# Moving one layer's hyena filter into its own layer in a two-layer encoder kernel

## The chip, the core and the metric

The kernel runs on one core of a Trainium2 chip. The metric is the device time of one execution in microseconds (us), from three runs, beside one profiled execution whose trace is read here. The names of the engines are those of the profile: PE (TensorE matmul) and PEld (its weight loads), DVE (VectorE), ACT (ScalarE), POOL (GpSimd), SP (SyncE, which here only issues loads).

## What is computed

Two requests ("streams" 0 and 1 below) of 512 tokens by 1024 channels go through two layers. The part of the reference that matters, cut:

```python
def _hyena_filters(L, w1, b1, freq, w2, b2, w3):       # depends on weights only, not on x
    feats = jnp.concatenate([t, jnp.cos(w), -jnp.sin(w)], axis=-1)          # 512 x 33
    h = jnp.sin(fr * (feats @ w1 + b1))                                     # 512 x 64
    h = jnp.sin(fr * (h @ w2 + b2))                                         # 512 x 64
    h = (h @ w3).reshape(L, HY_ORDER, 2, HY_WIDTH)                          # 512 x 1024
    h = h * jnp.exp(-t[:, :, None, None] * deltas)
    ...
    k_full = k_full / jnp.sum(jnp.abs(k_full), axis=0, keepdims=True)
    return jnp.fft.rfft(k_full, axis=0)

def _layer(x, p, ...):
    h = _rmsnorm(x, norm_mix)
    q, k, v, g, hy_in, pool_in = jnp.split(h @ w_in, ...)
    ret = _head_layernorm(_retention(q, k, v, ret_decay_fwd, ret_decay_bwd)) * silu(g)   # 4 heads of 128
    hy_out = _hyena(hy_in, ...)       # two long convolutions by FFT with the filters, 256 channels
    pool_out = _pool_mixer(pool_in, ...)
    x = x + jnp.concatenate([ret, hy_out, pool_out], -1) @ w_out
    gate, up = jnp.split(_rmsnorm(x, norm_ffn) @ ffn_w_up, 2, axis=-1)
    x = x + (gelu(_dwconv3(gate, ffn_conv)) * up) @ ffn_w_down
    return x + jax.nn.sigmoid(x @ ple_gate_w) * _rmsnorm(p @ ple_w, ple_norm)
```

The retention multiplies scores by a decay table exp(dist * log_sigmoid(logit)), one per head and layer, which also depends on weights only.

## The kernel before

Activations are held transposed, 128 channels by 512 tokens in a tile. Nearly every product is made in three float16 passes: both operands are split into a high and a low half (`split`: ACT writes the high half, DVE the low one), and high by high, high by low and low by high are summed. A projection of one 128-wide output tile is 24 matmuls. Weights arrive as `wraw` and are split into `wspl`.

One layer is a mixing block and a feed-forward block. In the mixing block the tiles come by `tile_order` (L100): four of retention's values (`v00` to `v11`, tiles `vp`), then head by head a query, a key and a gate (`q0`, `k0`, `g0`, ...), and between the heads the six hyena tiles `hy0` to `hy5` and the two pooling tiles `pl0`, `pl1`. Then come the eight tiles of the output projection, `o`, which contract over `mixr` (retention, four tiles), `mixh` (hyena, two) and `mixp` (pooling, two). The feed-forward block does both streams at once by a Strassen-like scheme (`fx`, `fy`, `fz`, `ex`, `ey`, `ez`).

The order of the instructions on PE and on SP is written out by hand. A planner in `schedule` runs generator threads: `main_thread` of each stream, and threads that they spawn, `head_thread` (scores `sc`, output `ov`, then sums of squares by `cs` and their broadcast by `rb`), `hyena_thread` (`tp` to token order, `sp` to the spectrum, products with the filter, `iv` back), `pool_thread`, `decay_thread` and `filter_thread`. A thread says after each step how long its next one should stay away (the table `LAT`); the planner takes the thread that is due on its own rough clock, which is no measured time, and what it emits first stands first on PE and on SP. The order on DVE, ACT and POOL is made by the framework's scheduler from the same program. Each engine takes its instructions strictly in its order.

`filter_thread` (L461) makes a layer's filter: features to 64 rows (`fp<-feats`), a sine, 64 rows again (`fp<-fa`), a sine, then eight products with `w3s` (the split of `w3`) with decay (`hfb`), absolute values (`fabs`) and their sum (`ftot`), one product with ones, a reciprocal (`frec`), folds (`fold`, `folds`), and nine products with cosine and sine matrices (`fp<-folds,fmat`), whose results are the tiles `khat`. A sine (L445) takes six DVE instructions of argument reduction on tile `fa` and its helper `sk`, then ACT's Sin. Layer 0's filter is started at the start. Layer 1's is started in layer 0, when stream 0 comes to `EARLY`, the tile `pl1`; its nine `khat` tiles are stored to DRAM (`ksp`) and loaded again in layer 1 by `load_dft` (L667).

`decay_thread` (L424) makes the decay tables: `log_sigmoid` (some 26 DVE instructions on 128x8), then eight sets of two DVE instructions and an Exp on tiles `dect`, each stored to DRAM. For layer l it is due at 25 + 400 l on the planner's clock, which puts layer 1's at the end of layer 0's mixing block.

The lines in the rows are those of these functions: L340 to L342 are the three passes of `pass3`, L335 to L337 those of `mm3`, L179 an ACT activation, L182, L185 and L189 the vector helpers, L766 `cs`, L776 `rb`.

Of the kernel before, what the change touches and what calls it, by code (L numbers as in the profile page):

```python
# [16 lines left out]
F32 = mybir.dt.float32  # L17
F16 = mybir.dt.float16
# [5 lines left out]
T = 512  # L24
# [27 lines left out]
EARLY = "pl1"  # L52
# [28 lines left out]
    "sin": (14.0, 17.0),  # L81
}
# [64 lines left out]
ORDERS = [tile_order(l in TWINNED) for l in range(DEPTH)]  # L147
# [7 lines left out]
class Trunk:  # L155
# [227 lines left out]
    def consts(self):  # L383
# [18 lines left out]
        self.ksp = self.dr.tile([9, 128, T], F32, name="ksp")  # L402
# [58 lines left out]
    def filter_thread(self, l, ev):  # L461
        nc, io = self.nc, self.io
        ft = self.g(name="feats")
        self.load(ft[0:33, :], io["feats"])
        fw = self.g(name="fw")
        self.load(fw[0:64, 0:132], io["fw"][l])
        w3 = []
        for o in range(2):
            w = self.g(name="w3")
            self.load(w[0:64, :], io["w3"][l][:, o * T:(o + 1) * T])  # L470
            q = self.g([128, 2, T], F16, name="w3s")
            self.split(q[0:64, 0], q[0:64, 1], w[0:64, :], WS)
# [4 lines left out]
        w1, w2, b1, fr, b2 = fw[0:33, 0:64], fw[0:64, 64:128], fw[0:64, 128:129], fw[0:64, 129:130], fw[0:64, 130:131]  # L477
        yield 0.0, 0.0
        a = self.g(name="fa")
        p = self.bank(name="fp")  # L480
        nc.tensor.matmul(p[0:64, :], w1, ft[0:33, :], start=True, stop=True)
        self.ts(a[0:64, :], p[0:64, :], b1, fr, ALU.add, ALU.mult)
        self.sine(a[0:64, :])
        yield 0.9, LAT["sin"][l > 0]
        a2 = self.g(name="fa2")
        p = self.bank(name="fp")
        nc.tensor.matmul(p[0:64, :], w2, a[0:64, :], start=True, stop=True)
        self.ts(a2[0:64, :], p[0:64, :], b2, fr, ALU.add, ALU.mult)
        self.sine(a2[0:64, :])
        a = None  # L490
        h2 = self.g([128, 2, T], F16, name="h2")
        self.split(h2[0:64, 0], h2[0:64, 1], a2[0:64, :])
        yield 0.9, LAT["sin"][l > 0]
# [62 lines left out]
        for i, (kind, pr, src) in enumerate(use):  # L556
# [19 lines left out]
        if l == 0:  # L576
            self.take_filters(kh)
# [993 lines left out]
```

## Time and profile before

| | |
|---|---|
| median of 3 runs | 2455.81 us (2454.49 to 2456.82) |
| profiled execution | 2456.78 us |
| its span, first to last instruction | 2455.0 us |
| PE busy | 2382.4 us, 97% |
| DVE busy | 1782.4 us, 73% |
| ACT busy | 1031.8 us, 42% |
| POOL busy | 710.3 us, 29% |
| PE's granted clock, mean | 0.989 |

The profiled execution lasted 1.78 us longer than its span. PE is busy nearly always, so the places where it is not are few and can be listed one by one; a timeline of PE gives, in square brackets, how long it stood idle before an instruction and which instruction on which engine ended the idle time. After a stop the granted clock is for a while at half (0.5 in the units of the profile, 1.2 of 2.4 GHz), which a view by windows shows as a mean under 1.

### The profile page before, as it was taken

How to read it: one execution, taken by the hardware profiler on the slowest of the kernel's cores; microseconds unless marked ns; L12 is line 12 of the kernel's file. 1: busy time of each engine (PE TensorE's matmuls, PEld its weight loads, DVE VectorE, ACT ScalarE, POOL GpSimd, SP SyncE). 2: the span in 40 equal slices, each digit the busy share in tenths (PEclk: the TensorE clock that was granted, in tenths of full speed). 3: DMA queues.
4: the chain of work that ended last, by engine and by line, in shares of the span. 5: the costliest groups of instructions: out<-in, count | busy, mean ns of one | idle time of the engine just before them, and what ended most of it. 6: DMA issues, size and time to landing. Idle time of an engine off the chain costs nothing.

```text
span 2455.0 us, 30870 instructions
## 1 busy us (share of the span) xinstructions
PE 2382.4 (97%) x12024; PEld 1172.0 (48%) x12024; DVE 1782.4 (73%) x2526; ACT 1031.8 (42%) x1551; POOL 710.3 (29%) x528
## 2 busy tenths in 40 slices
PE   5999999899999999999999999999999999999997
PEld 3544654444444444444456555544444444444443
DVE  7894886868877868866575686464887786986655
ACT  4553334334534525443533343332453453544441
POOL 1213343113333334330121223520423434332011
PEclk8999999999999999999999999999999999999999
DMA  6121020331121121113232111032012112111301
GB/s 225 65 98 62 25 75 11 117 129 43 50 64 60 50 71 48 60 52 114 72 127 91 67 45 51 35 115 65 18 55 66 57 47 69 54 58 52 112 1 69
DMA packets 64363, 168.60 MB, mean 69 GB/s; under 512 B 7574, under 2 KB 13718, under 8 KB 64216
## 3 DMA queue, kind: packets, MB, share of 16 engines
q1 hardware_dynamic: 58312, 156.40, 19.4%
q10 hardware_dynamic: 5904, 10.23, 1.1%
q8 instruction: 94, 1.54, 0.3%
q14 instruction: 53, 0.43, 0.1%
HBM read 152.18 MB, written 14.42 MB: 68 GB/s over the span
## 4 chain that ended last, share of the span: by engine, by line
PE 69%; DVE 7%; issue 2%; POOL 1%; ACT 1%; POOLq 0%; DVEq 0%; ACTq 0%
PE fx L1265 14%; PE ex L1265 7%; PE fy L1265 7%; PE ey L1265 4%; PE fz L1265 4%; PE s L335 2%; PE s L337 2%; PE s L336 2%; PE o L336 2%; PE ez L1265 2%; PE o L337 2%; PE o L335 2%; DVE conv L182 1%; PE d L335 1%; PE d L336 1%
## 5 line engine op out<-in xcount | busy, mean ns | idle before, releaser
L1265 PEld LDWEIGHTS <-wspl 128*128 128x128 f16 x4704 | 460.3, 98 | 559.1 <-issue 4.5
L185 POOL TENSOR_TENSOR wraw<-wraw 128x512 f32<-128x512 f32 (+1 forms) x240 | 350.2, 1459 | 641.1 <-DVE wspl L182 627.0
L179 ACT ACTIVATE wspl<-wraw 128x1024 f16<-128x1024 f32 (+2 forms) x360 | 326.8, 910 | 367.7 <-POOL wraw L185 76.0
L182 DVE SCALAR_TENSOR_TENSOR wspl<-wraw,wspl 128x1024 f16<-128x1024 f32 (+2 forms) x360 | 395.1, 1099 | 86.2 <-ACT wspl L179 84.8
L1265 PE MATMUL fx<-hs,wspl 128*128 128x512 f16 x1368 | 309.0, 379 | 3.6 <-ACT r L179 3.6
L335 PEld LDWEIGHTS <-wspl 128*128 128x128 f16 x1536 | 152.3, 99 | 182.3 <-issue 8.3
L337 PEld LDWEIGHTS <-wspl 128*128 128x128 f16 x1536 | 150.7, 98 | 184.5 <-issue 4.6
L336 PEld LDWEIGHTS <-wspl 128*128 128x128 f16 x1536 | 150.8, 98 | 183.3 <-issue 10.1
L1265 PE MATMUL ex<-at,wspl 128*128 128x512 f16 x846 | 192.7, 379 | 0.0
L185 POOL TENSOR_TENSOR y<-t,mhalf 128x4 f32<-128x4 f32 x30 | 38.7, 1290 | 411.1 <-DVE t L189 411.0
L179 ACT ACTIVATE at<-conv 128x512 f16<-128x512 f32 x142 | 88.4, 628 | 124.1 <-DVE conv L185 93.3
L182 DVE SCALAR_TENSOR_TENSOR conv<-r,scaled,conv 128x511 f32<-128x511 f32 x152 | 138.6, 912 | 2.4 <-ACT conv L179 0.8
L185 DVE TENSOR_TENSOR at<-conv,at 128x512 f16<-128x512 f32 x142 | 120.8, 854 | 23.3 <-ACT at L179 22.0
L179 ACT ACTIVATE conv<-conv 128x512 f32<-128x512 f32 x88 | 55.4, 629 | 126.5 <-DVE conv L182 125.4
L1265 PE MATMUL fx<-h,wspl 128*128 128x512 f16 x456 | 104.6, 379 | 0.0
L1265 PE MATMUL fy<-hs,wspl 128*128 128x512 f16 x456 | 104.6, 379 | 0.0
L1265 PE MATMUL fz<-h,wspl 128*128 128x512 f16 x456 | 104.6, 379 | 0.0
L1265 PE MATMUL fy<-h,wspl 128*128 128x512 f16 x456 | 104.6, 379 | 0.0
L179 ACT ACTIVATE sq<-x 128x512 f32<-128x512 f32 x80 | 49.0, 624 | 127.7 <-DVE x L182 69.3
L1265 PE MATMUL ey<-at,wspl 128*128 128x512 f16 x432 | 101.1, 379 | 0.0
L185 DVE TENSOR_TENSOR acc<-acc,sq 128x512 f32<-128x512 f32 x84 | 63.4, 756 | 49.1 <-ACT sq L179 47.8
L337 PE MATMUL s<-xs,wspl 128*128 128x512 f16 x256 | 97.0, 379 | 0.0
(246 smaller groups left out, 4676.1 us busy)
## 6 DMA issues: line engine op xcount, KB each, us to landing
wraw<-in_w SPq DMA_DIRECT2D x172, 512.0 KB, 3.7
wraw<-in_w SPq DMA_DIRECT2D x48, 384.0 KB, 3.0
x<-in_x SPq DMA_DIRECT2D x32, 256.0 KB, 4.2
dec<-ddec SPq DMA_DIRECT2D x16, 448.0 KB, 4.9
wraw<-in_w SPq DMA_DIRECT2D x16, 256.0 KB, 2.8
xsp<-x ACTq DMA_DIRECT2D x16, 256.0 KB, 2.0
x<-xsp SPq DMA_DIRECT2D x16, 256.0 KB, 4.6
out_y<-out SPq DMA_DIRECT2D x16, 256.0 KB, 2.2
```

Of the source, the lines that this page charges most:

```text
L179: return self.nc.scalar.activation(out=out, in_=in_, func=func, **k)
L182: return self.nc.vector.scalar_tensor_tensor(out=out, in0=in0, scalar=scalar, in1=in1, op0=op0, op1=op1)
L185: return (eng or self.nc.vector).tensor_tensor(out=out, in0=in0, in1=in1, op=op)
L335: self.nc.tensor.matmul(out, wv[:, 0, kb, :], x[:, 0], start=first, stop=False)
L336: self.nc.tensor.matmul(out, wv[:, 0, kb, :], x[:, 1], start=False, stop=False)
L337: self.nc.tensor.matmul(out, wv[:, 1, kb, :], x[:, 0], start=False, stop=last)
L1265: mm = lambda a, b, start=False, stop=False: self.nc.tensor.matmul(out, a, b, start=start, stop=stop, skip_group_check=not first)
```

## The change

- Layer 1's filter is started in layer 1 itself, when stream 1 comes to the tile `v10` of its mixing block. The trip through DRAM (nine stores, nine loads) is gone.
- The two sine layers of both layers' filters are computed at once in layer 0's filter thread: `fw` becomes block-diagonal, the products have 128 rows instead of 64, and the split result `h2` is kept; layer 1 takes its rows 64 to 127. The first sine's due time becomes 30 instead of 14 (`sin0`).
- In layer 1 the hyena tiles `hy0` to `hy3` come after `g1` instead of `g0`, and `hy4`, `hy5`, `pl0` and `pl1` after `g2`.
- In both layers the output projection contracts `mixh` and `mixp` first and `mixr` last.
- Layer 1's decay table is due at 25 + 625 on the planner's clock, in layer 0's feed-forward block.

The diff's core (the packing of `fw` in the same block-diagonal form is left out):

```diff
-EARLY = "pl1"
+EARLY = "v10"
+LATER = 625.0
...
     "sin": (14.0, 17.0),
+    "sin0": 30.0,
...
-def tile_order(twinned):
+def tile_order(layer, twinned):
...
-    for h, more in enumerate((["hy0", "hy1", "hy2", "hy3"], ["hy4", "hy5", "pl0"], ["pl1"], [])):
+    late = ([], ["hy0", "hy1", "hy2", "hy3"], ["hy4", "hy5", "pl0", "pl1"], [])
+    for h, more in enumerate(late if layer else (["hy0", "hy1", "hy2", "hy3"], ["hy4", "hy5", "pl0"], ["pl1"], [])):
...
     def sine(self, a):
-        k = self.g(name="sk")[0:64, :]
+        k = self.g(name="sk")
...
     def filter_thread(self, l, ev):
-        ft = self.g(name="feats")
-        self.load(ft[0:33, :], io["feats"])
-        fw = self.g(name="fw")
-        self.load(fw[0:64, 0:132], io["fw"][l])
+        rows = slice(l * 64, (l + 1) * 64)
+        if l == 0:
+            ft = self.g(name="feats")
+            self.load(ft[0:33, :], io["feats"])
+            fw = self.g(name="fw")
+            self.load(fw[:, 0:259], io["fw"])
...
-            self.split(q[0:64, 0], q[0:64, 1], w[0:64, :], WS)
+            self.split(q[rows, 0], q[rows, 1], w[rows, :], WS)
...
+        if l == 0:
+            w1, w2, b1, fr, b2 = fw[0:33, 0:128], fw[:, 128:256], fw[:, 256:257], fw[:, 257:258], fw[:, 258:259]
+            a = self.g(name="fa")
+            p = self.bank(name="fp")
+            nc.tensor.matmul(p, w1, ft[0:33, :], start=True, stop=True)
+            self.ts(a, p, b1, fr, ALU.add, ALU.mult)
+            self.sine(a)
+            yield 0.9, LAT["sin0"]
...
+            self.h2 = self.g([128, 2, T], F16, name="h2")
+            self.split(self.h2[:, 0], self.h2[:, 1], a2)
+            yield 0.9, LAT["sin"][0]
+        h2 = self.h2
...
-                self.pass3(p, h2[0:64, 0, jj], h2[0:64, 1, jj], w3[o][0:64, 0], w3[o][0:64, 1], True, True)
+                self.pass3(p, h2[rows, 0, jj], h2[rows, 1, jj], w3[o][rows, 0], w3[o][rows, 1], True, True)
...
-            if l > 0:
-                self.store(out=self.ksp[i], in_=kt)
-            else:
-                kh[kind, pr] = kt
+            kh[kind, pr] = kt
...
     def load_dft(self, l):
-        if l > 0:
-            kh = {}
-            for i, key in enumerate(FILTERS):
-                kh[key] = self.g(name="khat")
-                self.load(kh[key], self.ksp[i])
-            self.take_filters(kh)
...
             for name in MIXING[l]:
+                if name == EARLY and s == 1 and l > 0:
+                    self.spawn(self.filter_thread(l, self.khat_ev[l]))
...
-                if name == EARLY and s == 0 and l + 1 < self.depth:
-                    self.spawn(self.filter_thread(l + 1, self.khat_ev[l + 1]))
...
-                p = self._proj(l, f"o{m}", mix, s)
+                p = self._proj(l, f"o{m}", mix, s, order=(4, 5, 6, 7, 0, 1, 2, 3))
...
-            self.spawn(self.decay_thread(l, self.decay_ev[l])).ready = 25.0 + 400.0 * l
+            self.spawn(self.decay_thread(l, self.decay_ev[l])).ready = 25.0 + LATER * l
```

How this moves instructions is shown at three places, of the kernel before and of the changed one apart.

PE at the start of layer 0, around the second sine layer's product. Before it stands in the middle of the values of stream 0 (`vp`):

```order
L342 LDWEIGHTS h
L342 MATMUL vp<-wspl,h 128x256
L487 MATMUL fp<-fa,fw 64x512
L340 LDWEIGHTS h
L340 MATMUL vp<-wspl,h 128x256
```

PE at the same product in the changed kernel:

```order
L729 LDWEIGHTS h
L729 MATMUL vp<-wspl,h 128x256
L493 MATMUL fp<-fa,fw 128x512
L338 LDWEIGHTS wspl
L338 MATMUL g_883<-h,wspl 128x512
```

It now follows the values of stream 1 and precedes head 0's gate: one more half of the values of stream 0 (48 matmuls), `rb`, `q0`, `k0` and 96 matmuls of values of stream 1 have moved ahead of it.

DVE at the end of layer 0's mixing block, up to the last head's `mixr` before the output projection. Before, from the reciprocal of layer 1's filter on:

```order
L525 RECIPROCAL frec<-fp 128x512
L185 TENSOR_TENSOR rr<-rr,rb 128x512
L182 SCALAR_TENSOR_TENSOR wspl<-wraw,wspl 128x1024
L185 TENSOR_TENSOR mixr<-rr,mixr 128x512
L182 SCALAR_TENSOR_TENSOR rr<-ov,scaled_187,sg 128x512
L182 SCALAR_TENSOR_TENSOR x<-o_4214,x 128x512
L189 TENSOR_SCALAR t<-cs 128x4
L182 SCALAR_TENSOR_TENSOR wspl<-wraw,wspl 128x1024
L189 TENSOR_SCALAR rr_4283<-y 128x4
L185 TENSOR_TENSOR acc<-sq 128x512
L185 TENSOR_TENSOR fold<-fs_3673,fs_3675 128x512 x2
L185 TENSOR_TENSOR fold<-fd_3677,fd_3679 128x512 x2
```

It goes on with 18 more instructions of the filter and of layer 1's log-sigmoid before the last `rr<-rr,rb`, and more of both before the last `mixr`. DVE there in the changed kernel, from the last but one `mixr` to the last:

```order
L188 TENSOR_TENSOR mixr<-rr,mixr 128x512
L185 SCALAR_TENSOR_TENSOR rr<-ov,scaled_187,sg 128x512
L185 SCALAR_TENSOR_TENSOR wspl<-wraw,wspl 128x1024
L185 SCALAR_TENSOR_TENSOR x<-o_4057,x 128x512
L192 TENSOR_SCALAR t<-cs 128x4
L188 TENSOR_TENSOR acc<-sq 128x512
L192 TENSOR_SCALAR rr_4101<-y 128x4
L185 SCALAR_TENSOR_TENSOR rr_4101<-y,rr_4101 128x4
L185 SCALAR_TENSOR_TENSOR x<-o_4106,x 128x512
L185 SCALAR_TENSOR_TENSOR wspl<-wraw,wspl 128x1024
L188 TENSOR_TENSOR acc<-acc,sq 128x512
L185 SCALAR_TENSOR_TENSOR x<-o_4143,x 128x512
```

The next two of its rows are the last `rr<-rr,rb` and an `acc`, and then comes the last `mixr`. Nothing of the filter and of the log-sigmoid is left there.

PE in layer 1's mixing block, at the end of the third of the four `vp` groups of stream 1. Before, a hyena tile follows:

```order
L342 LDWEIGHTS h
L342 MATMUL vp<-wspl,h 128x256
L335 LDWEIGHTS wspl
L335 MATMUL hy_11194<-h,wspl 128x512
L336 LDWEIGHTS wspl
```

In the changed kernel the filter's first product with `w3s` follows that `vp` group (`h_870` is the `h2` kept from layer 0):

```order
L345 LDWEIGHTS h
L345 MATMUL vp<-wspl,h 128x256
L343 LDWEIGHTS h_870
L343 MATMUL fp<-w3s,h_870 128x512
L344 LDWEIGHTS h_870
```

DVE in the changed kernel from the end of that `vp` on (`mu`, `vc` and `v` belong to the values; the second step of `w3s` is DVE's half of the split):

```order
L748 TENSOR_REDUCE mu<-vp 128x4
L192 TENSOR_SCALAR mu<-mu 128x4
L185 SCALAR_TENSOR_TENSOR vc<-vp,mu 128x512
L188 TENSOR_TENSOR v<-vc,v 128x512
L185 SCALAR_TENSOR_TENSOR w3s<-w_10867,w3s 64x512
L185 SCALAR_TENSOR_TENSOR w3s<-w_10872,w3s 64x512
L188 TENSOR_TENSOR hfb<-fp,fdec 128x512
```

The split of `w3s` stands on DVE behind the four instructions that begin with the end of `vp`, and the product with `w3s` stands on PE directly behind `vp`.

## Rows read from the trace of the kernel before

**Rows 1.** Windows of the whole span: busy us (and instructions) of each engine, clock.

```profile
core 0: us, PE busy (x) PEld busy (x) DVE busy (x) ACT busy (x) POOL busy (x), PEclk, DMA share, GB/s
...
64.00:165.00 101.00, 97.95 (x550) 52.89 (x548) 93.04 (x175) 48.97 (x72) 24.42 (x18) 0.98 0.26 90
...
...
660.00:1286.00 626.00, 625.71 (x2975) 290.37 (x2974) 458.62 (x579) 273.70 (x402) 181.23 (x127) 1.00 0.22 71
1286.00:1640.00 354.00, 351.14 (x2073) 198.82 (x2072) 232.06 (x367) 135.13 (x208) 109.35 (x90) 1.00 0.19 64
```

**Rows 2.** Timeline of PE, layer 0: start, length, instruction [idle before it <-releaser].

```profile
53.93 1.96 PE L487 MATMUL fp<-fa,fw 64*64 64x512 f32 x2 [7.22 <-ACT fa L179]
...
152.72 0.55 PE L611 MATMUL tp<-ident,abs 128*128 128x128 f16 x4 [2.41 <-DVE abs L185]
...
287.97 0.28 PE L611 MATMUL tp<-ident,abs 128*128 128x128 f16 x2 [1.26 <-ACT abs L179]
...
297.54 0.27 PE L340 MATMUL sp<-u,fwd 128*128 128x256 f16 x1 [2.76 <-ACT u L179]
...
328.21 1.05 PE L766 MATMUL cs<-ones,sq 128*128 128x1 f32 x8 [2.95 <-ACT sq L179]
...
361.34 1.86 PE L766 MATMUL cs<-ones,sq 128*128 128x1 f32 x8 [2.86 <-ACT sq L179]
...
425.84 1.42 PE L766 MATMUL cs<-ones,sq 128*128 128x1 f32 x6 [2.75 <-ACT sq L179]
...
483.27 0.59 PE L335 MATMUL o<-mixr,wspl 128*128 128x512 f16 x1 [5.72 <-ACT mixr L179]
```

**Rows 3.** Windows around stops, columns as in rows 1 (PEclk is the eighth).

```profile
54.00:64.00 10.00, 10.00 (x59) 6.68 (x60) 5.86 (x10) 2.94 (x4) 0.00 (x0) 0.67 0.01 2
325.00:336.00 11.00, 8.05 (x35) 3.56 (x32) 7.68 (x16) 2.96 (x7) 2.49 (x2) 0.84 0.40 133
358.00:372.00 14.00, 11.14 (x39) 4.97 (x37) 9.29 (x16) 3.13 (x6) 6.64 (x5) 0.76 0.35 122
423.00:433.00 10.00, 7.25 (x23) 3.45 (x23) 8.25 (x17) 4.57 (x8) 3.65 (x3) 0.66 0.36 116
475.00:488.00 13.00, 6.82 (x24) 2.59 (x23) 12.70 (x37) 4.62 (x9) 0.00 (x0) 0.74 0.22 71
1608.00:1618.00 10.00, 8.29 (x35) 3.82 (x34) 7.73 (x13) 4.34 (x8) 3.47 (x3) 0.83 0.50 198
```

**Rows 4.** Timelines of DVE and PE around the first stop.

```profile
49.20 0.15 DVE L182 SCALAR_TENSOR_TENSOR rr<-y,rr 128x4 f16<-128x4 f32 x1
...
63.42 0.61 PE L776 MATMUL rb<-identr,rr 128*128 128x128 f16 x8
...
65.31 0.74 DVE L182 SCALAR_TENSOR_TENSOR hn<-x,vec,rb 128x512 f32<-128x512 f32 x1
```

**Rows 5.** Timelines of DVE, then PE: end of layer 0's mixing block; a product that goes.

```profile
450.64 3.36 DVE L525 RECIPROCAL frec<-fp 128x512 f32<-128x512 f32 x1 [0.17 <-PE fp L523]
...
463.59 3.43 DVE L185 TENSOR_TENSOR fold<-fs,fs 128x512 f32<-128x512 f32 x2
...
336.08 1.07 PE L481 MATMUL fp<-feats,fw 33*64 33x512 f32 x2
```

**Rows 6.** Timeline of ACT: a table load and the Sin behind it.

```profile
51.96 1.28 ACT L179 ACT_TABLE_LOAD   x1
53.25 0.63 ACT L179 ACTIVATE fa<-fa 64x512 f32<-64x512 f32 x1
```

**Rows 7.** Timelines of DVE and PE: layer 1, and PE in layer 0's feed-forward block.

```profile
1330.52 0.69 DVE L751 TENSOR_REDUCE mu<-vp 128x4 f32<-128x512 f32 x1 [3.32 <-PE vp L342]
...
1332.84 0.69 DVE L185 TENSOR_TENSOR v<-vc,v 128x512 f16<-128x512 f32 x1 [0.70 <-ACT v L179]
...
1612.89 1.13 PE L766 MATMUL cs<-ones,sq 128*128 128x1 f32 x8 [1.71 <-ACT sq L179]
...
652.88 1.46 PE L1265 MATMUL fx<-hs,wspl 128*128 128x512 f16 x6 [2.12 <-ACT r L179]
```

More of the change, by code (lines that the diff above doesn't have):

```diff
@@ L144, in step_time @@
     return 10.3
-ORDERS = [tile_order(l in TWINNED) for l in range(DEPTH)]
+ORDERS = [tile_order(l, l in TWINNED) for l in range(DEPTH)]
 TILES, MIXING = ORDERS[0][0], [o[2] for o in ORDERS]
@@ L401, in consts @@
         self.ddec = self.dr.tile([self.depth, HEADS, 128, 896], F32, name="ddec")
-        self.ksp = self.dr.tile([9, 128, T], F32, name="ksp")
         self.xsp = self.dr.tile([2, NB, 128, T], F32, name="xsp")
@@ L469, in filter_thread @@
             w = self.g(name="w3")
-            self.load(w[0:64, :], io["w3"][l][:, o * T:(o + 1) * T])
+            self.load(w[rows, :], io["w3"][l][:, o * T:(o + 1) * T])
             q = self.g([128, 2, T], F16, name="w3s")
-            self.split(q[0:64, 0], q[0:64, 1], w[0:64, :], WS)
+            self.split(q[rows, 0], q[rows, 1], w[rows, :], WS)
             w3.append(q)
@@ L476, in filter_thread @@
         self.load(bias, io["hbias"][l])
-        w1, w2, b1, fr, b2 = fw[0:33, 0:64], fw[0:64, 64:128], fw[0:64, 128:129], fw[0:64, 129:130], fw[0:64, 130:131]
         yield 0.0, 0.0
[L479 to L493, printed above, removed]
+        if l == 0:
[6 more added lines that the diff above has]
+            yield 0.9, LAT["sin0"]
+            a2 = self.g(name="fa2")
+            p = self.bank(name="fp")
+            nc.tensor.matmul(p, w2, a, start=True, stop=True)
+            self.ts(a2, p, b2, fr, ALU.add, ALU.mult)
+            self.sine(a2)
+            a = None
+            self.h2 = self.g([128, 2, T], F16, name="h2")
+            self.split(self.h2[:, 0], self.h2[:, 1], a2)
+            yield 0.9, LAT["sin"][0]
+        h2 = self.h2
         S = [self.g([128, 2, HYW], name=f"fs{j}") for j in range(4)]
@@ L569, in filter_thread @@
                 self.tt(kt, kt, bias, ALU.add, nc.gpsimd)
-            if l > 0:
-                self.store(out=self.ksp[i], in_=kt)
-            else:
-                kh[kind, pr] = kt
+            kh[kind, pr] = kt
             kt = src = None
             yield 1.3, 2.0
-        if l == 0:
-            self.take_filters(kh)
+        self.take_filters(kh)
         ev.set()
@@ L667, in load_dft @@
     def load_dft(self, l):
-        if l > 0:
-            kh = {}
-            for i, key in enumerate(FILTERS):
-                kh[key] = self.g(name="khat")
-                self.load(kh[key], self.ksp[i])
-            self.take_filters(kh)
         self.fwd, self.inv = [], []
@@ L1312, in schedule, with _proj @@
             t.step(self)
-    def _proj(self, l, nm, h, s, n=8):
+    def _proj(self, l, nm, h, s, n=8, order=None):
         p = self.bank(name=nm)
-        self.mm3(p, self.weight(l, nm, s), h, n=n)
+        self.mm3(p, self.weight(l, nm, s), h, n=n, order=order)
         return p
@@ L1529, in pack @@
     vec = np.zeros((depth, 128, V_END), f4)
-    fw = np.zeros((depth, 64, 132), f4)
+    fw = np.zeros((128, 259), f4)
     pw = np.zeros((depth, 128, 256), f4)
@@ L1541, in pack @@
         vec[l, :, V_LGB:V_LGB + 4] = a["ret_decay_bwd"][l][None]
-        fw[l, 0:33, 0:64] = a["hy_w1"][l]
-        fw[l, :, 64:128] = a["hy_w2"][l]
+        rows = slice(l * 64, (l + 1) * 64)
+        fw[0:33, rows] = a["hy_w1"][l]
+        fw[rows, 128 + l * 64:192 + l * 64] = a["hy_w2"][l]
         for k, n in enumerate(("hy_b1", "hy_freq", "hy_b2")):
-            fw[l, :, 128 + k] = a[n][l]
+            fw[rows, 256 + k] = a[n][l]
         for g in range(4):
```

## The prediction

> **What bounds the kernel now.** I read the windows by stage first. PE is busy for 625.71 of 626 us in layer 0's feed-forward block and DVE for 458.62 of them, ACT for 273.70 [rows 1]: PE bounds it there, and a change can only hurt. The time that can be won lies where PE stops, which is at the start, in layer 0's mixing block and, for a few us, in layer 1's. So the second view is PE's timeline, stop by stop [rows 2], and for each stop the engine that ended it. The eight rows of layer 0 add up to 27.9 us of idle time. The third view is the clock behind each stop: in 54 to 64 us PE never stops, yet the granted clock is 0.67 on the mean, so 10 x 0.33 = 3.3 us of full-clock work is lost [rows 3]. In the same way 11 x 0.16 = 1.8 us follow the stop at 328, 14 x 0.24 = 3.4 that at 361, and 10 x 0.34 = 3.4 that at 426 [rows 3]. Stops of 2.4 to 3 us thus cost nearly twice what the timeline says, and one that goes takes its slow stretch with it.
>
> The filter's DVE and ACT work is what several of these stops wait for, directly (`fa`) or as work standing ahead of `sq`, `u` and `mixr` on the same engines. The change takes one of the two filters out of layer 0 and pushes the other's sine back. In layer 1 DVE is busy 232.06 of 354 us [rows 1], so it has room.
>
> **The change part by part.** All sums start from the profiled execution, 2456.78 us, which is 0.97 above the median of the three runs.
>
> *The start.* PE stands 7.22 us before `fp<-fa` because the sine has not come through ACT, and then runs 3.3 us' worth slow [rows 2, 3]. In the new order 48 matmuls of `vp`, `rb`, `q0`, `k0` and 96 of `vp` of stream 1 come ahead of it. Are they ready? `rb` needs `rr`, done at 49.35, yet `rb` ran only at 63.42, being behind the stop; the chain of `hn` that feeds stream 1 began after it, at 65.31 [rows 4]. So everything moves up with PE. Ceiling: 7.22 + 3.3 = 10.5. From 64 to 165 us DVE is already busy 93.04 of 101 [rows 1] and can follow only so far: a part may come back as a longer stop at `tp` (2.41 now [rows 2]). I take **+9**, with 3 as the floor (7 us given back to DVE there). The stop at 152.72 itself I leave as it is, at 0.
>
> *The two 1.3 and 2.8 us stops at 288 and 297.5* (`tp`, `sp`, waiting for ACT's `abs` and `u`) [rows 2]: in the new order `ov` and a whole `pl`, some 8 us, come ahead of `tp`, and `sp` has more work before it. **+4**, between 0 and 4.
>
> *The stop at 328* has `sp`, `ov`, `iv`, `cs` in a row; the new order has `sp`, `iv`, `ov`, `q`, `cs`, one projection more. 2.95 + 1.8 = 4.7 at most; I take about half, **+2.5**, since the sums of squares still queue with the hyena products on DVE.
>
> *The stop at 361* comes while the sine of layer 1's filter stands on DVE ahead of the hyena products. That sine goes. 2.86 + 3.4 = 6.3 at most, 2 at least; **+5**.
>
> *The stop at 426.* Here filter products go from between the last heads, so PE loses filler as well as DVE loses work. The order left is that of layer 1's tail before, which stopped 1.71 and lost 10 x 0.17 = 1.7 by the clock [rows 3, 7]. 2.75 + 3.4 - 3.4 = **+2.7**, between 0 and 6.2.
>
> *The stop at 483.* PE waits 5.72 for the last `mixr` [rows 2]; in 475 to 488 us DVE is busy 12.70 of 13 [rows 3]. What fills it are the reciprocal (3.36), folds (two took 3.43) [rows 5], the products with `frec` and some 26 small instructions of log-sigmoid. All of these leave, and `mixr` is also contracted last. The window lost 13 x 0.26 = 3.4 by the clock, about half of it while PE stood. 5.72 + 1.7 = **+7.5**, at least 5.7: the surest term.
>
> *Work that goes.* Layer 1's own two small float32 products: 1.07 us for the pair of `fp<-feats` [rows 5], and about 1.0 for `fp<-fa` (1.96 at half clock [rows 2]): **+2.1**. The other filter products only change place, and 128 rows cost what 64 did, since the tiles' free size is the same 512.
>
> *The stores and loads of `ksp`* lay beside other work; 0.
>
> *Decay table in the feed-forward block.* Eight sets of `dect`, log-sigmoid, and table switches between Exp and the block's own functions: the written order has 21 table loads where it had 15, and one took 1.28 us [rows 6]: 6 x 1.28 = 7.7 us more on ACT, which is busy 273.70 of 626 [rows 1]. But the block's start already stops PE 2.12 us on ACT [rows 7], and log-sigmoid falls near it. **-1.5**, between 0 and -5 (two more stops of that size). The Trainium skill, "ScalarE: Activation LUTs", section "What ACT_TABLE_LOAD costs", adds some 1.38 us of drain to each load, which would make 16 us on ACT instead of 7.7. By that, I estimate -3 for this part in place of -1.5; the trace has the next activation begin 0.01 us behind a load (51.96 + 1.28, then 53.25 [rows 6]), so no drain shows there and I keep the lower price.
>
> *Layer 1's mixing block* pays. First, at the filter's start: `fp<-w3s` stands on PE directly behind a `vp`, and on DVE the split of `w3s` stands behind that `vp`'s own chain. In the old trace that chain starts at 1330.52, when `vp` ends, and is through at 1333.53 [rows 7]; one more split of 0.7 makes 1334.2. PE then stops 3.7 us, and loses some 1.8 by the clock as after the other stops: -5.5. Nothing of this depends on the load of `w3`; a late load would come on top. Second, the row `sp`, `ov`, `iv`, `cs` that stopped layer 0 at 328 now stands in layer 1: -(2.95 + 1.8) = -4.7. Third, its tail has `sc`, `rb`, `ov` without a projection between: -1, between 0 and -4. Against it, the old stop of 1.71 + 1.7 [rows 3, 7] belonged to an order that is gone: +3.4. Together **-7.8**, between -1 and -20. That the filter's eight products with `w3s` and nine with `fmat` stand between projections is filler that PE had elsewhere, and no new work.
>
> Sum: 9 + 4 + 2.5 + 5 + 2.7 + 7.5 + 2.1 = 32.8; less 1.5 and 7.8 gives 23.5, that is 2433.3. I say **2433**.
>
> **The rivals.**
>
> 1. *The start gives its gain back.* DVE is the limit until 165 us, so the stop at `tp` takes up what `fp<-fa` loses. For: 93.04 of 101 us busy [rows 1]. Against: it is the same work spread over a stretch that begins with an idle PE, and the second sine leaves this stretch's head. The gain falls from 9 to 1 or 2: about 2441.
>
> 2. *Layer 1 hands most of it back.* The filter makes hyena tiles and heads of layer 1 wait, a few stops of 3 + 1.8 us each as at 328. Three more than counted: 14 us, about 2447. For: three such stops stood in layer 0 with the same work [rows 2]. Against: DVE's room in layer 1 [rows 1]: with some 40 us of filter work on top, an estimate, 272 of 354.
>
> 3. *Slower.* One mechanism: PE takes its instructions in order, and `fp<-folds,fmat` in layer 1 stands behind `ftot`, reciprocal and folds. In layer 0's tail the reciprocal began at 450.64 and `mixr`, which stood behind part of the folds, let PE go only at 483.27 [rows 2, 5]: 33 us. In layer 1 some ten projections and smaller pieces, 50 us or more by the new order, lie between the product with ones and the first `fmat`. Only if the chain took 50 + 25 = 75 us there, over twice what it took in the most crowded place, would it eat the whole gain; at 85 us the time would be 2466. Against: DVE's room. The point from which it decides is that wait.
>
> 4. *All listed stops go* and layer 1 stops only for `w3s`: 10.5 + 4 + 4.7 + 6.3 + 6.2 + 7.5 + 2.1 - 5.5 gives 36: 2421. For: each of these stops has its named cause moved.
>
> *The change does not do what it says* is excluded for the order (it is written out), but the stops could be due to other work ahead on DVE; that is rivals 1 and 2.
>
> **How the numbers follow.** Forecast, 2426 to 2438: 0.60. Rival 1, 2438 to 2444: 0.14. Rival 2, 2443 to 2451: 0.11. Rival 4, 2416 to 2426: 0.11. Slower: 0.04. The range takes the forecast, rival 1, the nearer part of rival 2 and the greater part of rival 4: 2420 to 2446. The terms' own bounds fit: all at their floor except layer 1 would be 12.8 - 5 - 7.8, no change, which needs seven misses at once. A measurement of this kernel tells about 0.2%, 5 us, from no change. Faster by more than that (below 2450.9) is the forecast, rivals 1 and 4, and all but the end of rival 2: 0.93. Within it 0.03, slower 0.04.
>
> **What the profile of the changed kernel would show.** In layer 0: no stop before `fp<-fa`, `rb` of stream 1 near 52 us instead of 63.42 [rows 4], no long stop at 475 to 488 before `o<-mixr`, and DVE there far below 12.70 of 13. A stop at `tp` near 140 us of more than 5 us would mean rival 1. In layer 1: a stop of 3.5 to 4 us on DVE before the first `fp<-w3s`, followed by half clock, and one of about 3 us before a `cs`; several more of these, or one before `fp<-folds,fmat`, would mean rival 2 or 3. In the feed-forward block of layer 0: PE busy for over 624 us of 626; more idle time than 5 us there makes my price of the decay table wrong. The forecast is wrong outright if the sum of PE's idle time and clock losses before 500 us falls by less than 20 us.

## The result, and the profile after

The change makes the kernel slower: 2473.43 us median (2470.71 to 2477.33, six runs) beside 2454.51 (2454.48 to 2456.82, six runs); the ratio is 1.0073, 95% interval 1.0063 to 1.0083. The forecast was 2433, 2420 to 2446, with 0.04 for slower. The profiled execution of the changed kernel is the quickest of its six, 2470.71 us with a span of 2468.9.

First by stage. The borders are the same events in both kernels: the first `vp` of a layer, its first `o`, its first `fg`. Window rows of the kernel before, cut at its borders (length, then busy us and instructions of PE, PEld, DVE, ACT, POOL, then PEclk):

```profile
22.57:444.40 421.83, 394.52 (x2212) 216.80 (x2211) 326.34 (x558) 182.29 (x281) 131.87 (x105) 0.96 0.22 75
444.40:549.63 105.23, 99.05 (x475) 46.16 (x474) 80.07 (x136) 39.22 (x63) 18.78 (x13) 0.97 0.33 111
549.63:1276.10 726.47, 724.06 (x3395) 331.26 (x3394) 544.95 (x686) 324.43 (x482) 221.29 (x154) 1.00 0.21 66
1276.10:1628.01 351.91, 349.05 (x2102) 201.97 (x2101) 231.16 (x365) 134.35 (x208) 112.18 (x92) 1.00 0.20 67
```

The same of the changed kernel:

```profile
20.23:433.35 413.12, 384.03 (x2183) 214.99 (x2183) 304.29 (x503) 172.97 (x267) 131.27 (x105) 0.96 0.22 74
433.35:521.77 88.42, 88.42 (x437) 41.87 (x436) 43.41 (x65) 25.09 (x37) 5.49 (x5) 1.00 0.24 81
521.77:1249.13 727.36, 720.98 (x3378) 329.36 (x3377) 558.58 (x728) 337.13 (x497) 219.39 (x153) 1.00 0.20 67
1249.13:1643.30 394.17, 378.08 (x2202) 212.78 (x2201) 274.56 (x443) 151.22 (x240) 130.14 (x101) 0.98 0.18 60
```

Length less PE's busy time is the time PE stood; what the half clock cost is worked out from the same trace's clock records (busy time at half clock, times a half). The rest is work at full clock, which tells where instructions only moved:

| stage | before: stood + slow | work | after: stood + slow | work |
|---|---|---|---|---|
| up to layer 0's first `vp` | 17.8 + 0 | 4.8 | 15.3 + 0 | 4.9 |
| layer 0, mixing, to the first `o` | 27.3 + 15.2 | 379.4 | 29.1 + 13.1 | 370.9 |
| layer 0, output projection | 6.2 + 1.8 | 97.3 | 0 + 0 | 88.4 |
| layer 0, feed-forward | 2.4 + 0 | 724.1 | 6.4 + 0 | 721.0 |
| layer 1, mixing, to the first `o` | 2.9 + 1.7 | 347.3 | 16.1 + 7.2 | 370.9 |
| layer 1, output projection | 0 + 0 | 88.4 | 0 + 0 | 85.4 |
| the rest, to PE's last instruction | 7.0 + 0.6 | 721.9 | 7.6 + 1.5 | 722.2 |

In both kernels another 9.0 us follow PE's last instruction.

The columns of work add up to 2363 us before and 2364 after: the 2.1 us of products that go do not show at this size, and the filter's work only changes place, out of layer 0 into layer 1's mixing block. So the 13.9 us between the spans are stops and slow clock: 2.5 won ahead of the first `vp`, nothing in layer 0's mixing block (42.5 and 42.2), 8.0 won at its output projection, 4.0 lost in the feed-forward block, 18.7 in layer 1's mixing block and 1.5 in the rest.

The stops themselves, in PE's timeline of the changed kernel (answering rows 2 and 7; an instruction without brackets did not wait):

```profile
49.83 0.61 PE L773 MATMUL rb<-identr,rr 128*128 128x128 f16 x8
71.12 1.02 PE L493 MATMUL fp<-fa,fw 128*128 128x512 f32 x2
123.45 0.38 PE L338 MATMUL hy<-h,wspl 128*128 128x512 f16 x1 [1.58 <-DVE hfb L188]
141.03 1.22 PE L530 MATMUL fp<-ftot,ones 128*128 128x512 f32 x1 [3.41 <-DVE ftot L188]
179.35 0.58 PE L343 MATMUL ov<-pt,v 128*128 128x512 f16 x1 [3.58 <-ACT pt L182]
311.96 1.87 PE L763 MATMUL cs<-ones,sq 128*128 128x1 f32 x8 [5.30 <-ACT sq L182]
332.27 0.38 PE L338 MATMUL q<-h,wspl 128*128 128x512 f16 x1 [1.85 <-DVE t L188]
362.60 1.86 PE L763 MATMUL cs<-ones,sq 128*128 128x1 f32 x8 [5.54 <-ACT sq L182]
419.91 1.05 PE L763 MATMUL cs<-ones,sq 128*128 128x1 f32 x8 [1.64 <-ACT sq L182]
561.74 0.38 PE L339 MATMUL fg<-h,wspl 128*128 128x512 f16 x1 [2.72 <-POOL h L188]
1306.52 0.37 PE L343 MATMUL fp<-w3s,h 64*128 64x512 f16 x1 [3.02 <-ACT w3s L182]
1391.96 1.87 PE L763 MATMUL cs<-ones,sq 128*128 128x1 f32 x8 [6.71 <-ACT sq L182]
1509.44 1.87 PE L763 MATMUL cs<-ones,sq 128*128 128x1 f32 x8 [2.85 <-ACT sq L182]
```

The stop before `fp<-fa` is gone, and `rb` comes at 49.83 instead of 63.42 [rows 4]: the start did move up by 13.6 us. The stops at 288 and 297.5 are gone too (a `hy` that waits 0.58 us at 282.16 is the longest left between 200 and 305 us). But new ones stand before `fp<-ftot`, `ov` and `q`, and those before `cs<-sq` are longer: 22.1 us in sum over the whole run, 10.9 before.

### The profile page after: what moved, and what is told of

It is laid out like the page before. It is cut to its first block, busy times and chain, and to the rows that moved or that the text cites. A ratio compares the mean times of both kernels' runs of the same rounds, so it can differ in the third digit from the quotient of the medians.

```text
span 2468.9 us, 30852 instructions
## 1 busy us (share of the span) xinstructions
PE 2385.5 (97%) x12020; PEld 1174.2 (48%) x12020; DVE 1775.5 (72%) x2511; ACT 1035.0 (42%) x1554; POOL 709.2 (29%) x528
## 3 DMA queue, kind: packets, MB, share of 16 engines
q1 hardware_dynamic: 56956, 154.04, 18.7%
## 4 chain that ended last, share of the span: by engine, by line
PE 76%; DVE 15%; issue 3%; ACT 3%; POOL 3%; DMA 1%; SPq 0%; POOLq 0%; ACTq 0%; DVEq 0%
PE fx L1262 12%; PE ex L1262 7%; PE fy L1262 6%; PE ey L1262 4%; PE fz L1262 3%; DVE conv L185 2%; PE o L338 2%; PE o L340 2%; PE o L339 2%; DVE wspl L185 2%; PE s L338 2%; PE s L340 2%; PE s L339 2%; PE ez L1262 2%; DVE t L188 2%
## 5 line engine op out<-in xcount | busy, mean ns | idle before, releaser
L188 POOL TENSOR_TENSOR sw<-sw,rope 128x512 f32<-128x512 f32 x32 | 44.5, 1392 | 195.6 <-ACT sw L182 195.5
```

Source lines behind the costliest of these rows:

```text
L188: return (eng or self.nc.vector).tensor_tensor(out=out, in0=in0, in1=in1, op=op)
```

## The experiments

Three suspects: the sine's due time, the decay table's, and the spacing of the heads' sums (`cs`) behind their outputs (`ov`). The first four runs undo or alter one part of the changed kernel at a time. Each group of four was measured beside the kernel before, whose medians there are 2454.06, 2455.12 and 2455.82 us (2454.51 beside the changed kernel); differences between times of different groups are uncertain by up to 1.8 us for that.

**The sine's due time alone put back.**

```diff
-    "sin0": 30.0,
+    "sin0": 14.0,
```

> The changed kernel with the first sine's due time back at 14 instead of 30 (one number in LAT). Theory A (DVE is the limit of the first 180 us, and late filter steps collide with head 1): the stop before fp<-fa of some 7 us comes back, the stops before fp<-ftot (3.4) and ov<-pt (3.6 + 0.9) and their slow stretches shrink, the sum of idle time before 200 us stays within 4 us of the changed kernel's, and the time is within 5 us of 2473. Rival (the stops at ftot and ov<-pt have nothing to do with where the sine went): they stay and the 7 us come on top, about 2480 or more.

Measured: 2460.32 us (2457.03 to 2463.96), 13.1 less than the changed kernel; ratio to before 1.0024 (1.0014 to 1.0034). PE's timeline and a line of its waits:

```profile
51.65 2.08 PE L493 MATMUL fp<-fa,fw 128*128 128x512 f32 x2 [6.44 <-ACT fa L182]
...
PE cs L763 <- ACT sq L182: 13.3, 4, 6.7
```

The stop at the start is back, as both theories said, and with it the stops at `tp` (3.17 at 150 and 1.34 at 285 us) and `sp` (2.76 at 295) that the kernel before has; the time falls all the same. The stops at `ov` (3.58 and 0.90) go, and 2.5 of the 3.41 at `ftot`, and 8.8 of the 22.1 us before `cs`. The stops between the first `vp` and 200 us sum to about the same, as the first theory had it (14.2 and 13.1), but neither expected time holds, because the gain comes later: idle and slow time in layer 0's mixing block falls from 42.2 to 33.3 us. The later sine, which I had put down as the largest gain, costs some 13 us.

**The decay table alone put back.**

```diff
-LATER = 625.0
+LATER = 400.0
```

> The changed kernel with layer 1's decay table due at 25 + 400 again; PE's order is the same, word for word. Theory A (decay work stops PE in the feed-forward block): idle time from layer 0's fg to layer 1's vp falls from 6.4 to about 2.4 us, the output projection of layer 0 stays without a stop because the filter's DVE work is gone from there, and the time falls by about 4 us to 2469. Rival (log-sigmoid alone refills the end of layer 0's mixing block): a stop of 2 to 4 us before o<-mixr, time unchanged.

Measured: 2466.52 us (2465.46 to 2470.34), 6.9 less than the changed kernel; in the profiled executions 4.6 less, of which this stage has 3.8. The window of layer 0's feed-forward block:

```profile
521.13:1244.44 723.31, 720.76 (x3377) 329.26 (x3376) 545.59 (x691) 323.38 (x481) 220.60 (x153) 1.00 0.20 64
```

PE stands 2.55 us there, not 6.38, and the output projection still has no stop. PE's order is the same in both kernels, so this is the decay table's own price. The stop of 2.72 before `fg` at 561.74 falls to 0.71.

**Layer 1's tiles in the old order.**

```diff
-    for h, more in enumerate(late if layer else ([...])):
+    for h, more in enumerate(late if False else ([...])):
```

> The changed kernel with layer 1's tiles in the old order (hy0 to hy3 after g0, and so on). Theory A (the stops before cs are collisions of one head's ov, sq, cs chain with a burst of hyena or filter work standing ahead of sq on ACT and DVE, so they depend on the order and not on the load): the stops of 6.7 and 2.9 us in layer 1 go to other places and change size, total of layer 1's idle time and clock loss anywhere between 12 and 30 us, 23 now; the 3 us before fp<-w3s stay. Rival (load: the filter needs the later hyena tiles to be ahead of the spectrum): more stops, before sp or yt or fp<-folds, and 5 to 15 us slower.

Measured: 2483.27 us (2480.38 to 2487.02), 9.8 more. Layer 1's mixing block by window, and one of its stops:

```profile
1253.61:1657.48 403.87, 381.21 (x2181) 212.88 (x2180) 270.11 (x434) 148.58 (x236) 123.32 (x101) 0.96 0.17 58
...
1533.71 1.87 PE L763 MATMUL cs<-ones,sq 128*128 128x1 f32 x8 [5.11 <-ACT sq L182]
```

PE stands 22.7 us and loses 13.2 by the clock, 36 in all, above the first theory's 12 to 30; the time is the rival's. But the stops are not where the rival wanted them, before `sp`, `yt` or the products with `fmat`: with layer 0's tile order, layer 1 has layer 0's stops, 5.11, 5.54 and 1.67 before `cs` where layer 0 has 5.30, 5.55 and 1.66 in the same run. The two layers are not loaded alike (DVE 304.33 of 415 us in layer 0 of this run, 270.11 of 404 here). The stops follow the order.

**More room between `ov` and `cs`.**

```diff
-    "ov": (2.6, 5.0),
+    "ov": (2.6, 9.0),
```

> The changed kernel with LAT ov 9 instead of 5, so that each head's sums cs come about one projection later on PE behind ov. Theory A (collisions ahead of sq on ACT): idle time before cs<-sq falls from 22.1 to under 10 us and the time by 12 to 20 us, to 2453 to 2461. Rival (DVE and ACT are short of time there, and cs is only the first to show it): the stops move to rb, tp, iv or o, and the time falls by less than 5 us.

Measured: 2455.72 us (2453.82 to 2457.17), 17.7 less; ratio to before 1.0005 (0.9996 to 1.0015). No stop before `cs<-sq` is left of the 22.1 us. The gain is layer 0's: idle and slow time of its mixing block falls from 42.2 to 26.1 us. Layer 1's mixing block has other stops instead, 26.1 us beside 23.3, the longest of them this:

```profile
1530.95 0.37 PE L343 MATMUL sp<-u,fwd 128*128 128x256 f16 x1 [9.43 <-ACT u L182]
```

The planner there put this spectrum in two halves around an inverse, with one `pl` between `tp` and the first half. On ACT its `u` began at 1529.89, behind a `qk` that had waited 3.00 us for POOL's `rt`.

The next four ask what is left of the change when its two late due times are put back, and whether the spacing is the cause in the kernel before too.

**Both due times put back.**

```diff
-    "sin0": 30.0,
+    "sin0": 14.0,
...
-LATER = 625.0
+LATER = 400.0
```

> The changed kernel with the sine's due time back at 14 and the decay table back at 25 + 400: the filter's move, the joint sines, the new tile order and the new contraction order are what is left of the change. PE's order is that of the run with the sine alone put back (2460.3). Theory A (the decay table's price in the feed-forward block is its own, 4 to 7 us, whatever the rest does): 2453 to 2456, no difference from the kernel before, with 18 to 19 us of idle time and clock loss more in layer 1's mixing block and as much less in layer 0. Rival (the decay work refills the end of layer 0): no gain over 2460.

Measured: 2457.37 us (2455.79 to 2460.03); ratio to before 1.0009 (1.0000 to 1.0019), which a measurement here cannot tell from none. The decay table is worth 3.0 us beside the sine (3.6 in its own stage), a little under what was expected. In layer 0's mixing block and output projection PE stands or runs slow 34.3 us instead of 50.5, in layer 1's mixing block 23.4 instead of 4.6: 16 won, 19 paid. The stop at 361 is gone here, that at 328 has 2.90 of its 2.95 us left and that at 426 has 1.67; those at 288 and 297.5 are back at 1.34 and 2.76.

**The same with the spacing at 7.**

```diff
-    "ov": (2.6, 5.0),
+    "ov": (2.6, 7.0),
```

> As the run before, with LAT ov 7 instead of 5. Theory A (stops before cs<-sq are a matter of how far cs stands behind ov on PE): the four stops before cs<-sq, 13.3 us with some 6 to 7 us of slow clock behind them, fall under 4 us and the time is 2436 to 2443. Rival (other stops take their place, as a 9.4 us stop before sp did with LAT ov 9): 2446 to 2455.

Measured: 2448.00 us (2445.65 to 2449.68), ratio to before 0.9967 (0.9954 to 0.9980). The stops before `cs<-sq` fall from 13.3 to 4.0 as the theory said, yet the time is the rival's: 9.4 us less, where 14 to 21 were expected. By stage, layer 0's and layer 1's mixing blocks win 8.7 and 6.7 us of idle and slow time, and 3.2 of it goes again in layer 0's feed-forward block (1.5 us of stops and 1.7 of slow clock more).

**The kernel before with the spacing at 7.**

```diff
-    "ov": (2.6, 5.0),
+    "ov": (2.6, 7.0),
```

> The kernel before with LAT ov 7 instead of 5 and nothing else. Theory A (the stops at 328, 361 and 426 us come from the small distance of cs behind ov and not from layer 1's filter): their 8.6 us and most of their slow clock go, 2440 to 2448. Rival (they come from the filter's work on DVE, as the prediction had it): they stay over 5 us in sum, and the time is within 4 us of 2454.5.

Measured: 2444.58 us (2442.74 to 2444.99), ratio 0.9952 (0.9937 to 0.9967). The three `cs` that waited 2.95, 2.86 and 2.75 us [rows 2], and wait no more:

```profile
330.29 0.95 PE L766 MATMUL cs<-ones,sq 128*128 128x1 f32 x8
...
360.30 0.95 PE L766 MATMUL cs<-ones,sq 128*128 128x1 f32 x8
...
420.89 0.95 PE L766 MATMUL cs<-ones,sq 128*128 128x1 f32 x8
```

Layer 1's filter, its sine and its decay table are all still in layer 0 here. So these stops need not wait for the filter to leave: more room behind `ov` takes them away with all of that work in place. In the last stretch, though, other stops have come, one of them before a product of the filter itself:

```profile
406.85 0.61 PE L340 MATMUL ov<-pt,v 128*128 128x512 f16 x1 [2.29 <-DVE st L182]
...
436.01 0.67 PE L523 MATMUL fp<-ftot,ones 128*128 128x512 f32 x1 [3.43 <-DVE ftot L185]
```

From 400 us to layer 0's first `o`, PE's idle and slow time is 9.1 us, 6.2 in the kernel before.

**The kernel before with the contraction order alone.**

```diff
-                p = self._proj(l, f"o{m}", mix, s)
+                p = self._proj(l, f"o{m}", mix, s, order=(4, 5, 6, 7, 0, 1, 2, 3))
```

> The kernel before with the output projection contracting mixh and mixp first, in both layers, and nothing else. Theory A (the last mixr is late because filter and log-sigmoid stand ahead of it on DVE): putting mixr last hides only the half projection that goes ahead, some 2.7 of the 6.2 us, and the time falls by 2 to 4 us. Rival (the contraction order alone removes that stop): 6 to 8 us less, 2446.5 to 2448.5.

Measured: 2453.53 us (2450.21 to 2455.82), ratio 0.9993 (0.9983 to 1.0002): no difference that can be told, where the first theory expected 2 to 4 us less. The stop at `mixr`:

```profile
478.22 0.38 PE L335 MATMUL o<-mixr,wspl 128*128 128x512 f16 x1 [3.13 <-ACT mixr L179]
```

With 0.67 behind it, 3.8 us are left of 6.2, so 2.4 of it can be hidden behind the half projection that now goes ahead, as the first theory said of the stop; the rest went only where the filter's DVE work had gone or the spacing was larger.

The last four: the stop at `w3s` by itself, and the best that each place of the filter gives.

**Layer 1's `w3` loaded and split at `v00`.**

```diff
+                if name == "v00" and s == 1 and l > 0:
+                    self.w3 = self.split_w3(l)
                 if name == EARLY and s == 1 and l > 0:
                     self.spawn(self.filter_thread(l, self.khat_ev[l]))
```

> The changed kernel with layer 1's w3 loaded and split when stream 1 comes to v00 instead of v10; PE's order is the same, word for word, and on DVE the splits now stand ahead of the last vp's own chain. Theory A (the 3.0 + 0.4 us stop before fp<-w3s is the split standing behind that chain): the stop goes with the slow clock behind it, 4 to 6 us less, 2467 to 2470. Rival (the load of w3 is what is late, or the next stop before cs takes the gain up): the stop stays, or cs at 1392 grows from 6.7 by as much; 2471 to 2475.

Measured: 2466.69 us (2464.15 to 2472.36), 6.7 less than the changed kernel (4 to 6 were expected). The first product with `w3s`, no longer waiting:

```profile
1304.33 0.39 PE L343 MATMUL fp<-w3s,h 64*128 64x512 f16 x1
```

Of layer 1's mixing block, stops and slow clock fall from 23.3 to 18.7 us, and the 6.71 us before `cs` stay as they were. That is 4.6 in this stage, and the stop stands by itself.

**The kernel before with the spacing at 7 and the contraction order.** (Both diffs as above.)

> The kernel before with LAT ov 7 and with mixh and mixp contracted first. Theory A (the rest of the stop before o<-mixr, 2.0 us with ov 7, is what the contraction order can hide): 2440 to 2444, no stop over 0.5 us before o<-mixr. Rival (the stop is that of another instruction by then): 2444 to 2446.

Measured: 2441.11 us (2440.49 to 2441.39), ratio 0.9941 (0.9926 to 0.9956). The stop before `o<-mixr` is gone.

**The same with the joint sines, layer 1's filter still in layer 0.** (`filter_thread` as in the change; started at `pl1` of stream 0, khat through DRAM, old tile order, decay table at 25 + 400.)

> LAT ov 7, mixh and mixp first, and the joint sines, but layer 1's filter stays in layer 0 where it was before (from pl1 of stream 0, through DRAM), old tile order, decay table at 25 + 400. Theory A (moving the filter into layer 1 is what costs; the joint sines are worth their 2.1 us of products and some DVE time): 2436 to 2442, faster than the same spacing with the filter in layer 1 (2448). Rival (it is DVE at the end of layer 0 that costs, and the filter there still stops PE): 2444 to 2452.

Measured: 2447.09 us (2445.93 to 2449.76), 6.0 more than without the joint sines: the rival. With its sines done ahead, layer 1's filter runs through its products sooner, and stops again at `w3s` (3.71 and 2.10) and most of all here:

```profile
437.17 0.61 PE L343 MATMUL sc<-qk 128*128 128x512 f16 x1 [8.46 <-ACT qk L182]
```

**The filter in layer 1 with every repair.**

```diff
-    "sin0": 30.0,
+    "sin0": 14.0,
...
-LATER = 625.0
+LATER = 400.0
...
-    "ov": (2.6, 5.0),
+    "ov": (2.6, 7.0),
```

(with `w3` split at `v00` as above.)

> The filter in layer 1 as in the change, with every repair together: sine at 14, decay table at 25 + 400, LAT ov 7, w3 split early; PE's order is that of the run that gave 2448.0. Theory A (independent terms): 4 to 6 us less than 2448.0, that is 2442 to 2444, with 4.7 us of cs<-sq and small stops left in layer 1. Rival (the time won at w3s is lost at the next stop, 3.75 us before cs): 2446 to 2449.

Measured: 2441.90 us (2440.38 to 2442.50), ratio 0.9943 (0.9927 to 0.9960); 6.1 less than 2448.00 for the early split. Layer 1's mixing block:

```profile
1233.64:1616.03 382.39, 373.86 (x2210) 211.30 (x2209) 272.48 (x443) 151.25 (x241) 128.48 (x101) 1.00 0.18 62
```

PE stands 8.5 us there and loses 1.7. This and the kernel before with the spacing and the contraction order both beat the kernel before by 0.6% (the changed kernel by 1.3%), and cannot be told from each other. So the best version that was run with the filter in layer 1 is no faster than the best with it in layer 0. That the place by itself makes no difference is not shown: the two also differ in the joint sines, the tile order and the early split.

## Why the prediction was wrong

In layer 0's mixing block the forecast had five terms that sum to +23.2. PE's idle and slow time there, by stretch (the stops of the kernel before in brackets):

| stretch | forecast gain | before | after | both due times put back | kernel before, spacing 7 |
|---|---|---|---|---|---|
| first `vp` to 200 us (54, 153) | +9 | 20.6 | 20.3 | 20.3 | 18.3 |
| 200 to 305 us (288, 297.5) | +4 | 4.9 | 0.6 | 6.1 | 6.6 |
| 305 to 345 us (328) | +2.5 | 4.7 | 11.0 | 4.6 | 0 |
| 345 to 400 us (361) | +5 | 6.1 | 8.8 | 0 | 0.3 |
| 400 us to the first `o` (426) | +2.7 | 6.2 | 1.6 | 3.4 | 9.1 |

That is 0.3 won where 23.2 were forecast: 23 of the 37 us between the forecast and the profiled execution. Another 11 are layer 1's mixing block. The 2.1 of products that go do not show, and the 2.5 won ahead of the first `vp` and 1.5 lost in the rest were in no term.

**The start, +9.** The stop went and `rb` moved up by 13.6 us, more than counted. The step that failed is what follows from it: "everything moves up with PE". Moved later on PE, the filter's steps met head 1 on DVE and ACT (`ftot` 3.41, `ov<-pt` 3.58), and the slow clock behind these two stops cost 3.1 and 2.2 us: up to 200 us, 0.4 was won and not 9. And the planner laid the hyena groups and heads otherwise, which gave 5.30 and 5.54 before `cs`. With the due time alone put back, these two stops are 2.04 and none, and the kernel is some 13 us faster. Rival 1 had the direction, "the start gives its gain back", at a price of 8; the sign was beyond it.

**The stops at 288, 328, 361 and 426, +14.2 together.** Two of the four terms came true at their place: those at 288 and 297.5 went, and at 426 a stop of 1.64 is left where 1.71 was forecast, without the slow clock. The main error lies at 328 and 361, where the new orders stop longer than the old. "One projection more" was the reason for +2.5: in the row `sp`, `iv`, `ov`, `q`, `cs`, though, `q` only takes the place that `iv` had between `ov` and `cs`. PE has 5.18 us of work there, 5.24 before, and this `cs` is the one that waits 5.54. (The kernel before has `iv`, `ov`, `q`, `cs` too, at its stop of 361.) And the `ov` and `pl` that came ahead of `tp` and took the stops at 288 and 297.5 away put that head's `cs` behind `ov`, `pl`, `tp`, 6.07 us behind its `ov`: it waits 5.30, and the forecast had no price for it. On ACT, `sq` stands between the two, behind a hyena step that waits for DVE:

```profile
310.79 0.63 ACT L182 ACTIVATE abs<-ab 128x512 f16<-128x512 f32 x1 [4.11 <-DVE ab L188]
311.33 0.58 ACT L182 ACTIVATE sq<-ov 128x512 f32<-128x512 f32 x1
...
361.43 0.63 ACT L182 ACTIVATE mixh<-yv 128x512 f16<-128x512 f32 x1 [2.50 <-DVE yv L185]
361.97 0.58 ACT L182 ACTIVATE sq<-ov 128x512 f32<-128x512 f32 x1
```

`ov` was done at 300.58 and 351.87, so `sq` began 10.8 and 10.1 us behind it, and `cs` stood 6.07 and 5.18 behind it on PE. In the kernel before with more room behind `ov`, `cs` stands 10.3 and 11.3 us behind, and the stops at 328 and 361 are gone while the filter's sine is still there.

"That sine goes" was the reason for +5 at 361. It named one of the works ahead of `sq` and took it for the only one: in the changed kernel the sine is gone from there, and what ACT has ahead of `sq` are hyena steps. With both due times put back, the sine is gone too and this `cs` does not wait; but the order around it has changed as well, so what the sine alone was worth is not shown. A new order decides which heads are hit.

**The stop at 483, +7.5.** Right: 6.2 + 1.8 before, none after. In 464 to 477 us, where it would stand now, DVE is busy 4.43 of 13 us (12.70 in rows 3):

```profile
464.00:477.00 13.00, 13.00 (x62) 5.90 (x61) 4.43 (x6) 2.84 (x4) 0.00 (x0) 1.00 0.34 119
```

**The decay table, -1.5.** Right in sign, too small: 4.0 by stage, and putting it back gave 3.6 and 3.8 by stage (3.0 and 6.9 in time), near the far end of the bounds. The estimate of -3, from the price of a switch in the Trainium skill, "ScalarE: Activation LUTs", section "What ACT_TABLE_LOAD costs", comes nearer, but no drain shows in the trace: the load at 544.20 begins 0.07 us behind the step before it, and the next step 0.01 us behind the load. The six loads more lie on ACT, while the longest new stop, 2.72 before `fg`, waits for POOL's `h`.

**Layer 1's mixing block, -7.8.** It cost 18.7, inside the bounds I gave the term (-1 to -20). Two pieces were right: the stop at `w3s`, forecast at 3.7 + 1.8, is 3.02 + 0.42 with 1.7 of slow clock, and 4.6 went in this stage when it was taken away; and the `cs` behind `sp`, `ov`, `iv`, forecast at 2.95 + 1.8 as in layer 0, is 2.85 + 3.2. The piece that I did not see is 6.71 us at 1391.96 with 2.2 of slow clock. The rows on DVE, POOL and ACT between `ov` and that `cs`:

```profile
1371.73 3.34 DVE L532 RECIPROCAL frec<-fp 128x512 f32<-128x512 f32 x1
...
1387.15 0.67 DVE L188 TENSOR_TENSOR rt<-q,rope 128x512 f32<-128x512 f32 x1
...
1385.96 2.61 POOL L188 TENSOR_TENSOR sw<-sw,rope 128x512 f32<-128x512 f32 x1 [18.96 <-ACT sw L182]
1388.65 1.59 POOL L188 TENSOR_TENSOR rt<-rt,sw 128x512 f32<-128x512 f32 x1
...
1384.04 0.63 ACT L182 ACTIVATE folds<-fold 128x512 f16<-128x512 f32 x1 [5.46 <-DVE fold L188]
1384.69 1.19 ACT L182 ACTIVATE sw<-q 64x512 f32<-64x512 f32 x2
1390.28 0.63 ACT L182 ACTIVATE qk<-rt 128x512 f16<-128x512 f32 x1 [4.39 <-POOL rt L188]
1390.81 0.61 ACT L182 ACTIVATE folds<-fold 128x512 f16<-128x512 f32 x1
1391.33 0.58 ACT L182 ACTIVATE sq<-ov 128x512 f32<-128x512 f32 x1
```

`ov` is done at 1380.07 and one hyena tile stands on PE between it and `cs`. On ACT, `sq` stands behind `qk`, and `qk` waits for POOL's two rotation steps. The first, `sw`, could start only behind ACT's `sw<-q`, which stood behind the filter's `folds`, for which ACT had waited 5.46 us. The second, `rt`, is that of a query whose DVE half came at 1387.15, behind the reciprocal and the products with `frec`. By these rows it is the filter's own burst that makes `sq` late here. I had said that DVE has room in layer 1, on the mean: 232 of 354 us [rows 1], 244.57 after. That is so, and it says nothing of a burst of 16 us in one place. The forecast priced layer 1 by its load; it is an order problem there too. More room shortens this stop and does not end it at once: with the spacing at 7 it is 3.75 us.

**The rivals.** Rival 2, layer 1 hands most of it back, is what happened there: 10.9 us more than counted, against its 14, at a chance of 0.11. Rival 3, slower through the products with `fmat` waiting, did not happen: no stop before `fp<-folds,fmat` is in the trace. The kernel became slower because layer 0's mixing block gave back all that it was to win, more than rival 1 had priced, while layer 1 paid as rival 2 had it; I had priced the two as alternatives to each other. My own test for a forecast wrong outright, idle and slow time before 500 us falling by less than 20, is met: 68.2 us before and 57.5 after (50.5 and 42.2 without the stretch up to the first `vp`).

What stays open is why the joint sines cost 6 us with the filter in layer 0. The trace of that run shows the pattern of 1391.96 again: ahead of the stop of 8.46, ACT's `folds` had waited 7.11 us for DVE's `fold`, and `sw` and `qk` stand behind it. But no run took that stop away by itself.

## What to carry to other kernels

A stop whose releaser is the last of a queue on an in-order engine has two cures: more distance between its producer and its consumer, or less work ahead of the step between them. The row that names the releaser does not say how much of the queue one piece of that work makes up. Before a stop is put on the side of gains, count PE's work between producer and consumer in the new order (a tile that takes another's place adds none), and try the distance alone, which here was one number and gave 10.5 us. When an edit re-lays a hand-written order, count the old stops of that kind as still there, at other places, until an experiment shows otherwise; and judge an engine's room by the burst between two dependent instructions, not by its busy share over a stage.

## What the runs showed of the hardware

Not every stop was followed by half clock. Behind 2.95 us before `cs` at 328.21, in the kernel before, the granted clock fell to 0.5 and 1.7 us of work were lost; behind 2.76 us before `sp` at 297.54 in the same trace, and behind 2.72 us before `fg` at 561.74 in that of the changed kernel, it stayed at 1.00.

The spread of a kernel's runs goes with the granted clock. Of the six runs of the changed kernel the four quickest, from 2470.71 us, have a mean clock of 0.987 or 0.988, the two slowest, 2477.24 and 2477.33, have 0.985 and 0.984; four runs of the version with the least idle and slow time (the kernel before with the spacing at 7 and the contraction order) stay between 2440.49 and 2441.39 at 0.991 to 0.992. So here the kernel with more stops is also less even, and its runs lie further apart (6.6 us) than most terms of the sum are large.

POOL's rotation step slows down beside some of DVE's two-input steps. `sw<-sw,rope` took 2.61 us at 1385.96, while DVE ran products with `frec`, whose two inputs are both in SBUF; and 1.27 us here, where one input of each DVE step beside it (`q`, `sp`) is a matmul's result in PSUM:

```profile
342.81 1.27 POOL L188 TENSOR_TENSOR sw<-sw,rope 128x512 f32<-128x512 f32 x1 [6.74 <-ACT sw L182]
...
342.76 0.69 DVE L188 TENSOR_TENSOR rt<-q,rope 128x512 f32<-128x512 f32 x1
343.37 1.34 DVE L188 TENSOR_TENSOR t<-sp,khat 128x256 f32<-128x256 f32 x3
```

The Trainium skill, "SBUF — State Buffer", section "Who interferes with whom", says that a DVE instruction with two SBUF inputs contends with a GpSimd instruction that reads SBUF. The rows agree. What the 1.3 us were worth in the longest stop of layer 1 is less: `rt` needed DVE's half too, which ended at 1387.82, so by these rows at most 0.8 us of them lay on the chain.
